# Multiplying gamma into all four chunks of the last row block ahead of its root, on GpSimd and VectorE

## The chip, the cores and the metric

The kernel runs on one core of a Trainium2 chip. The metric is the device time of one execution in microseconds (us). Every kernel was run, and one execution of each was profiled. The profile names the engines PE (TensorE), DVE (VectorE), ACT (ScalarE), POOL (GpSimd) and SP (the engine that issues most DMAs here). "Chunk" means 512 of the 2048 columns of a block of 128 rows.

## The reference

```python
m, k, n = 2048, 2048, 2048          # a, b, gamma: float32
x = np.matmul(a, b)
rms = np.sqrt(np.mean(x ** 2, axis=-1, keepdims=True) + eps)
return (gamma * x / rms).astype(np.float32)
```

A row of the output cannot be scaled before the whole row of x is known, because its rms needs all 2048 columns.

## The kernel before

The kernel computes the product by a scheme of seven products for each pair of row blocks, keeps x in SBUF, and finishes each block with `x * r * gamma`, where r is one over the rms. ("The root" below is the step on ScalarE that makes the rms; "filler" is work put where VectorE would otherwise wait for it.) The change touches only the very last block of 128 rows, `rb`, whose root comes after the last matmul. This is the end of the kernel:

```python
# gam[c]: chunk c of gamma; xb: chunks 0 and 1 of the last rows, x22[0] is chunk 1
# x21[1], x22[1]: places of chunks 2 and 3; p4[1]: chunk 2, still in PSUM
def add(out, in0, in1, op=ALU.add):
    nc.vector.tensor_tensor(out=out, in0=in0, in1=in1, op=op)
def scaled_gamma(x, src, r, gamma_of_x):
    nc.vector.scalar_tensor_tensor(out=x, in0=src, scalar=r, in1=gamma_of_x,
                                   op0=ALU.mult, op1=ALU.mult)
def by_r(x, r):
    nc.scalar.activation(out=x, in_=x, func=ACTF.Copy, scale=r)
# ... cut: the seven products; chunk 0 is already multiplied by gam[0] ...
add(x22[0], p6, t[0])
square(rb, x22[0])
scaled_gamma(x_tile(ra, 1), x_tile(ra, 1), r_a, gamma_sb[:, HALF:])
nc.sync.dma_start(out=rows(ra, HALF, N), in_=x_tile(ra, 1))
# ... cut: the last products, in two halves of 256 columns ...
for h, col in enumerate(halves):
    add(x22[1][:, col], p6[h], t[1][:, col])
    # ... cut: ScalarE squares this half and sums it into half_sq[:, h] ...
# ... cut: part = half_sq[:, 0:1] + the sums of the other chunks ...
add(x22[0], x22[0], gam[1], ALU.mult)          # filler while ScalarE makes the root
r_b = inverse_rms(half_sq[:, 1:2], part)       # ScalarE root, VectorE reciprocal
x = xb[:, 0:CH]
nc.vector.tensor_scalar_mul(out=x, in0=x, scalar1=r_b)
nc.sync.dma_start(out=rows(rb, 0, CH), in_=x)
x = xb[:, CH:]
by_r(x, r_b)
nc.scalar.dma_start(out=rows(rb, CH, HALF), in_=x)
for c, x, src in ((3, x22[1], x22[1]), (2, x21[1], p4[1])):
    scaled_gamma(x, src, r_b, gam[c])
    nc.sync.dma_start(out=rows(rb, c * CH, (c + 1) * CH), in_=x)
```

Of the kernel before, what the change touches and what calls it, by code (L numbers as in the profile page):

```python
# [8 lines left out]
FP32 = mybir.dt.float32  # L9
# [4 lines left out]
ALU = mybir.AluOpType  # L14
# [3 lines left out]
def kernel(  # L18
# [13 lines left out]
    nc = tc.nc  # L32
    P = 128
    M, K = a.shape
# [5 lines left out]
    CH = 512  # L40
    NCH = N // CH
    HALF = N // 2
# [6 lines left out]
    a_pool = ctx.enter_context(tc.tile_pool(name="a_pool", bufs=2))  # L49
# [61 lines left out]
    a32 = {}  # L111
# [134 lines left out]
    def b_quarter(j, kp, r, c):  # L246
        return raw[j][kp][:, r, c * CH:(c + 1) * CH]
# [24 lines left out]
    def product(g, j, m, bank, start=True):  # L272
        for kp in range(KP):
            lhsT = {3: quarter(g, 0, 0), 4: quarter(g, 1, 1)}[m] if m in (3, 4) else s_sum[m]
            rhs = {1: lambda: sums[j][:, 0, kp, :], 2: lambda: b_quarter(j, kp, 0, 0),
                   3: lambda: sums[j][:, 1, kp, :], 4: lambda: sums[j][:, 2, kp, :],
                   5: lambda: b_quarter(j, kp, 1, 1), 6: lambda: b_quarter(j, kp, 0, 1),
                   7: lambda: b_quarter(j, kp, 1, 0)}[m]()
            nc.tensor.matmul(bank, lhsT[:, kp, :], rhs,  # L279
                             start=(start and kp == 0), stop=(kp == KP - 1),  # L280
                             skip_group_check=not start)
# [5 lines left out]
    def square(mb, src):  # L287
        c = n_sq[mb]
        n_sq[mb] += 1
        sq = sq_pool.tile([P, 2 * CH], BF16, name="sq")  # L290
        nc.scalar.activation(out=sq[:, 0:CH], in_=src, func=ACTF.Square,  # L291
                             scale=inv_sqrt_n, accum_out=msq[mb][:, c:c + 1])

    def x_tile(mb, h):


        if (mb, h) not in x_half:
            n = n_x[0]
            n_x[0] += 1
            if n < 8:  # L300
                slot = n
            else:
                g = n // 4
                slot = ((0, 4, 1, 5), (0, 1, 4, 5))[g // 2 % 2 == 0][n % 4] + 2 * (g % 2)
            x_half[mb, h] = x_slot[slot]
        return x_half[mb, h]

    def x_chunk(mb, c):
        return x_tile(mb, c // 2)[:, (c % 2) * CH:(c % 2 + 1) * CH]
# [21 lines left out]
    def rows(mb, lo, hi):  # L331
        return out[mb * P:(mb + 1) * P, lo:hi]

    def finish(mb, order=(0, 1)):
        if mb not in rms_of:
            take_rms(mb)
        r = inverse(rms_of.pop(mb))
        for h in order:
            x = x_half.pop((mb, h))
            nc.vector.scalar_tensor_tensor(  # L340
                out=x, in0=x, scalar=r, in1=gamma_sb[:, h * HALF:(h + 1) * HALF],
                op0=ALU.mult, op1=ALU.mult)
            nc.sync.dma_start(out=rows(mb, h * HALF, (h + 1) * HALF), in_=x)
# [9 lines left out]
    def new_bank():  # L353
        return ps_a.tile([P, CH], FP32, name="acc")
# [123 lines left out]
    def last_squares():  # L478

        while late:  # L480
            square(*late.pop(0))
# [109 lines left out]
    def last_group():  # L591


        g = NG - 1
        ra, rb = 2 * g, 2 * g + 1
        x11, x12, x21, x22 = ([x_chunk(mb, 2 * j + c) for j in range(2)]
                              for mb in (ra, rb) for c in range(2))
        xa, xb = x_tile(ra, 0), x_tile(rb, 0)
        gam = [gamma_sb[:, c * CH:(c + 1) * CH] for c in range(NCH)]
        gam_left = gamma_sb[:, 0:HALF]  # L600
        t = x22

        def partial(mb):

            m = msq[mb]
            part = stat_pool.tile([P, 1], FP32, name="part")
            nc.vector.tensor_scalar(out=part, in0=m[:, 0:1], scalar1=m[:, 1:2],
                                    scalar2=m[:, NCH:], op0=ALU.add, op1=ALU.add)
            return part

        def plus(part, mb, c):
            both = stat_pool.tile([P, 1], FP32, name="both")
            nc.vector.tensor_tensor(out=both, in0=part, in1=msq[mb][:, c:c + 1], op=ALU.add)
            return both
# [11 lines that stand above are left out]
        p4 = []  # L626
        for j in range(2):
            p5, p1 = new_bank(), new_bank()
            p4.append(new_bank())
            product(g, j, 5, p5)  # L630
            nc.scalar.copy(out=t[j], in_=p5)
            last_squares()
            product(g, j, 1, p1)
            add(t[j], p1, t[j], ALU.subtract)
            if j == 0:
                finish(2 * g - 2)
            product(g, j, 4, p4[j])
            nc.scalar.copy(out=x21[j], in_=p4[j])
            add(x11[j], t[j], x21[j])
            if j == 0:  # L640
                finish(2 * g - 1)
            product(g, j, 3, p5, start=False)
            nc.scalar.copy(out=x12[j], in_=p5)
            square(ra, x12[j])
            add(t[j], x11[j], x12[j])
            p7 = new_bank()
            product(g, j, 7, p7)
            add(x11[j], p7, x11[j])
            square(ra, x11[j])
            if j == 0:  # L650
                product(g, j, 2, p4[j], start=False)
                nc.scalar.copy(out=x21[j], in_=p4[j])
                square(rb, x21[j])
                add(t[j], t[j], x21[j], ALU.subtract)
                pre_a = partial(ra)
                add(xa, xa, gam_left, ALU.mult)
                add(x21[j], x21[j], gam[0], ALU.mult)
        r_a = inverse_rms(msq[ra][:, NCH - 1:NCH], plus(pre_a, ra, 2))
        by_r(xa, r_a)
        nc.sync.dma_start(out=rows(ra, 0, HALF), in_=xa)  # L660
        p6 = new_bank()
        product(g, 0, 6, p6)
        add(x22[0], p6, t[0])
        square(rb, x22[0])
        scaled_gamma(x_tile(ra, 1), x_tile(ra, 1), r_a, gamma_sb[:, HALF:])
        nc.sync.dma_start(out=rows(ra, HALF, N), in_=x_tile(ra, 1))
        product(g, 1, 2, p4[1], start=False)
        add(t[1], t[1], p4[1], ALU.subtract)
        square(rb, p4[1])
        pre_b = partial(rb)  # L670

        half_sq = stat_pool.tile([P, 2], FP32, name="n2")
        halves = [slice(0, CH // 2), slice(CH // 2, CH)]
        p6 = [new_bank()[:, 0:CH // 2] for _ in halves]
        for bank, col in zip(p6, halves):
            for kp in range(KP):
                nc.tensor.matmul(bank, s_sum[6][:, kp, :], b_quarter(1, kp, 0, 1)[:, col],
                                 start=(kp == 0), stop=(kp == KP - 1))
        for h, col in enumerate(halves):
            add(x22[1][:, col], p6[h], t[1][:, col])  # L680
            sq = sq_pool.tile([P, 2 * CH], BF16, name="sq")
            nc.scalar.activation(out=sq[:, 0:CH // 2], in_=x22[1][:, col], func=ACTF.Square,  # L682
                                 scale=inv_sqrt_n, accum_out=half_sq[:, h:h + 1])
        part = stat_pool.tile([P, 1], FP32, name="part")
        nc.vector.tensor_scalar(out=part, in0=half_sq[:, 0:1], scalar1=pre_b,
                                scalar2=msq[rb][:, 2:3], op0=ALU.add, op1=ALU.add)
        add(x22[0], x22[0], gam[1], ALU.mult)
        r_b = inverse_rms(half_sq[:, 1:2], part)
        x = xb[:, 0:CH]
        nc.vector.tensor_scalar_mul(out=x, in0=x, scalar1=r_b)  # L690
        nc.sync.dma_start(out=rows(rb, 0, CH), in_=x)
        x = xb[:, CH:]
        by_r(x, r_b)
        nc.scalar.dma_start(out=rows(rb, CH, HALF), in_=x)
        for c, x, src in ((3, x22[1], x22[1]), (2, x21[1], p4[1])):
            scaled_gamma(x, src, r_b, gam[c])
            nc.sync.dma_start(out=rows(rb, c * CH, (c + 1) * CH), in_=x)

    for g in range(G0, NG - 1):
        for j in range(2):  # L700
# [36 lines left out]
```

## Time and profile before

| | |
|---|---|
| Time of the kernel before | 224.7 us median of 3 runs (224.52 to 224.71) |
| Profiled span | 222.6 us |
| Reciprocal of the last rows starts | 216.16 us |
| First and last of the four stores issued | 216.87 and 218.19 us |
| Last packet of the last store | 221.06 us (from the trace's record of DMA packets) |

The page's first part gives each engine's busy time, with its share of the span in brackets and the number of its instructions:

```profile
PE 211.1 (95%) x1043; PEld 98.6 (44%) x1043; DVE 161.8 (73%) x324; ACT 129.1 (58%) x272; POOL 24.5 (11%) x49
```

PE fills the span up to the last matmul, and the change does not touch it. What it touches is the stretch after it. Here is the timeline of that stretch. Its columns are the start in us, the duration in us, the engine, the line of the source, the operation, what it writes and reads with the shapes, the count, and in brackets the idle time before it with its releaser:

```profile
214.72 0.42 DVE L617 TENSOR_TENSOR x<-acc,x 128x256 f32<-128x256 f32 x1 [0.26 <-PE acc L677]
215.29 0.42 ACT L682 ACTIVATE sq<-x 128x256 bf16<-128x256 f32 x1
215.48 0.68 DVE L617 TENSOR_TENSOR x<-x,gamma_sb 128x512 f32<-128x512 f32 x1
215.83 0.29 ACT L328 ACTIVATE rms<-n,part 128x1 f32<-128x1 f32 x1
216.16 0.16 DVE L322 RECIPROCAL r<-rms 128x1 f32<-128x1 f32 x1
216.35 0.72 ACT L624 ACTIVATE x<-x,r 128x512 f32<-128x512 f32 x1 [0.23 <-DVE r L322]
216.35 0.48 DVE L690 TENSOR_SCALAR x<-x,r 128x512 f32<-128x512 f32 x1
216.76 0.74 DVE L620 SCALAR_TENSOR_TENSOR x<-x,r,gamma_sb 128x512 f32<-128x512 f32 x1
216.87 0.33 SPq L691 DMA_DIRECT2D out_dram<-x  x1
217.11 0.36 ACTq L694 DMA_DIRECT2D out_dram<-x  x1
217.42 0.74 DVE L620 SCALAR_TENSOR_TENSOR x<-acc,r,gamma_sb 128x512 f32<-128x512 f32 x1
217.53 1.05 SPq L697 DMA_DIRECT2D out_dram<-x  x2
```

The half add at 214.72 is the last thing that waits for a matmul. From there a serial path leads through the square, the root and the reciprocal. Then four chunks are scaled and stored, and VectorE's two instructions of 0.74 us are the longest part of it. The chain of waits says the same: its last pieces (start, duration, what) are these.

```profile
216.35 0.48 DVE x L690
216.84 0.66 DVEq L732
217.50 0.66 DVE x L620
```

This invites the reading that 0.66 us of VectorE work is worth removing. But the chain shown here stops at the last compute instruction, at 218.16, while the span goes on for 4.4 us. The busy time by stretches shows what fills them. Its last two columns are the busy share of the core's 16 DMA engines and what they moved, in GB/s:

```profile
core 0: us, PE busy (x) PEld busy (x) DVE busy (x) ACT busy (x) POOL busy (x), PEclk, DMA share, GB/s
217.50:218.00 0.50, 0.00 (x0) 0.00 (x0) 0.50 (x2) 0.00 (x0) 0.00 (x0) 1.00 0.59 217
218.00:218.50 0.50, 0.00 (x0) 0.00 (x0) 0.16 (x1) 0.00 (x0) 0.00 (x0) 1.00 1.04 385
218.50:219.00 0.50, 0.00 (x0) 0.00 (x0) 0.00 (x0) 0.00 (x0) 0.00 (x0) 1.00 1.05 340
219.00:219.50 0.50, 0.00 (x0) 0.00 (x0) 0.00 (x0) 0.00 (x0) 0.00 (x0) 0.82 1.12 316
219.50:220.00 0.50, 0.00 (x0) 0.00 (x0) 0.00 (x0) 0.00 (x0) 0.00 (x0) 0.50 0.98 332
220.00:220.50 0.50, 0.00 (x0) 0.00 (x0) 0.00 (x0) 0.00 (x0) 0.00 (x0) 0.50 1.08 324
220.50:221.00 0.50, 0.00 (x0) 0.00 (x0) 0.00 (x0) 0.00 (x0) 0.00 (x0) 0.50 0.49 184
```

From 218.0 on the DMA engines are full (a share of 1.0; it can exceed 1 because the recorded times of packets overlap), and they stay full until about 220.4.

### The profile page before, as it was taken

How to read it: one execution, taken by the hardware profiler on the slowest of the kernel's cores; microseconds unless marked ns; L12 is line 12 of the kernel's file. 1: busy time of each engine (PE TensorE's matmuls, PEld its weight loads, DVE VectorE, ACT ScalarE, POOL GpSimd, SP SyncE). 2: the span in 40 equal slices, each digit the busy share in tenths (PEclk: the TensorE clock that was granted, in tenths of full speed). 3: DMA queues.
4: the chain of work that ended last, by engine and by line, in shares of the span. 5: the costliest groups of instructions: out<-in, count | busy, mean ns of one | idle time of the engine just before them, and what ended most of it. 6: DMA issues, size and time to landing. Idle time of an engine off the chain costs nothing.

```text
span 222.6 us, 3026 instructions
## 1 busy us (share of the span) xinstructions
PE 211.1 (95%) x1043; PEld 98.6 (44%) x1043; DVE 161.8 (73%) x324; ACT 129.1 (58%) x272; POOL 24.5 (11%) x49
## 2 busy tenths in 40 slices
PE   7899999999999999999999999999999999999950
PEld 2445444444454444444444444444444444444430
DVE  2427557983999989978949298837994589587692
ACT  3110002807698895799646985699478954334570
POOL 7534232300000001000100002000200000000000
PEclk9999999999999999999999999999999999999997
DMA  6999999999973499818889259945994794044045
GB/s 184 223 202 209 203 208 211 212 303 259 327 280 159 188 272 292 310 72 226 276 228 400 58 174 222 366 151 143 246 368 168 97 282 189 0 188 193 0 190 188
DMA packets 36176, 47.13 MB, mean 212 GB/s; under 512 B 21952, under 2 KB 26048, under 8 KB 34496
## 3 DMA queue, kind: packets, MB, share of 16 engines
q0 software_dynamic: 9648, 23.33, 41.6%
q1 hardware_dynamic: 26080, 22.29, 33.0%
q10 hardware_dynamic: 432, 1.31, 2.0%
q8 instruction: 8, 0.13, 0.2%
q14 instruction: 8, 0.07, 0.1%
HBM read 34.60 MB, written 16.78 MB: 231 GB/s over the span
## 4 chain that ended last, share of the span: by engine, by line
PE 83%; DMA 8%; DVE 2%; POOL 2%; issue 1%; ACT 1%; DVEq 0%; ACTq 0%; POOLq 0%
PE acc L279 63%; PE acc L350 18%; DMA b<-in_b_dram 8%; POOL early L106 1%; DVE x L617 1%; POOL b L100 1%; DVE x L620 1%; PE tbank L179 1%; PE tbank L382 1%; PE tbank L165 1%; ACT sq L291 0%; DVEq L732 0%; ACT sq L682 0%; DVE x L690 0%; DVE r L322 0%
## 5 line engine op out<-in xcount | busy, mean ns | idle before, releaser
L279 PE MATMUL acc<-b,s 128*128 128x512 bf16 x376 | 83.3, 379 | 0.0
L279 PEld LDWEIGHTS <-s 128*128 128x128 f16 x472 | 46.2, 98 | 55.7 <-DVE s L244 0.2
L350 PE MATMUL acc<-b,head_at 128*128 128x512 bf16 x240 | 55.1, 379 | 0.6 <-DMA b<-in_b_dram 0.4
L291 ACT ACTIVATE sq<-x 128x512 bf16<-128x512 f32 x62 | 39.1, 631 | 10.9 <-DVE x L520 5.1
L340 DVE SCALAR_TENSOR_TENSOR x<-x,r,gamma_sb 128x1024 f32<-128x1024 f32 x28 | 34.7, 1282 | 0.8
L209 ACT ACTIVATE sq<-a 128x1024 bf16<-128x1024 f32 x24 | 25.4, 1057 | 16.8 <-DMA a<-in_a_dram 16.4
L350 PEld LDWEIGHTS <-head_at 128*128 128x128 bf16 x240 | 22.9, 98 | 26.7 <-issue 1.1
L393 ACT COPY x<-acc 128x512 f32<-128x512 f32 x11 | 5.9, 591 | 25.1 <-PE acc L350 25.1
L231 ACT ACTIVATE head_at<-a,s 128x2048 f16<-128x2048 f32 x10 | 19.9, 1990 | 0.0
L279 PEld LDWEIGHTS <-at_even 128*128 128x128 f16 x96 | 9.4, 98 | 11.5 <-issue 0.4
L279 PEld LDWEIGHTS <-head_at 128*128 128x128 f16 x96 | 9.4, 98 | 11.3
L100 POOL DMA_DIRECT2D b<-in_b_dram x15 | 10.6, 708 | 16.0 <-DMA b<-in_b_dram 13.2
L217 DVE TENSOR_SCALAR s<-norm 128x1 f32<-128x1 f32 x12 | 1.8, 150 | 14.3 <-ACT norm L212 14.2
L244 DVE TENSOR_TENSOR s<-at_even 128x1024 f16<-128x1024 f16 x15 | 9.7, 684 | 2.8 <-DMA at_even<-head_at 2.8
L291 ACT ACTIVATION_READ_ACCUMULATOR sq<-x 128x1 f32 x62 | 11.7, 188 | 0.0
L279 PE MATMUL acc<-t_left,s 128*128 128x512 bf16 x48 | 11.3, 379 | 0.0
L279 PE MATMUL acc<-early,s 128*128 128x512 bf16 x48 | 11.3, 379 | 0.0
L279 PE MATMUL acc<-early,at_even 128*128 128x512 bf16 x48 | 11.0, 379 | 0.0
L279 PE MATMUL acc<-t_left,at_even 128*128 128x512 bf16 x48 | 10.9, 379 | 0.0
L509 ACT COPY x<-acc 128x512 f32<-128x512 f32 x10 | 5.7, 575 | 8.9 <-PE acc L279 8.9
L279 PE MATMUL acc<-t_left,head_at 128*128 128x512 bf16 x48 | 10.8, 379 | 0.0
L279 PE MATMUL acc<-early,head_at 128*128 128x512 bf16 x48 | 10.8, 379 | 0.0
(86 smaller groups left out, 205.8 us busy)
## 6 DMA issues: line engine op xcount, KB each, us to landing
out_dram<-x SPq DMA_DIRECT2D x30, 512.0 KB, 3.1
a<-in_a_dram POOLq DMA_DIRECT2D x12, 1024.0 KB, 8.5
b<-in_b_dram POOLq DMA_DIRECT2D x15, 512.0 KB, 17.1
early<-in_a_dram POOLq DMA_DIRECT2D x7, 256.0 KB, 14.8
early<-in_b_dram ACTq DMA_DIRECT2D x2, 512.0 KB, 5.9
gamma_sb<-in_gamma_dram POOLq DMA_DIRECT2D x1, 1024.0 KB, 19.9
out_dram<-x SPq DMA_DIRECT2D x3, 256.0 KB, 3.5
early<-in_a_dram SPq DMA_DIRECT2D x1, 512.0 KB, 5.7
```

The lines of the kernel that those rows point to most:

```text
L100: nc.gpsimd.dma_start(out=raw[j][kp], in_=b[kp * W2:(kp + 1) * W2, j * HALF:(j + 1) * HALF].rearrange("(t p) n -> p t n", p=P))
L106: nc.gpsimd.dma_start(out=ah(kp), in_=a[0:HB * P, kp * W2:(kp + 1) * W2].rearrange("(r p) k -> p r k", p=P))
L165: nc.tensor.matmul(view[:, t, r, :], ah(kp)[:, r, t * P:(t + 1) * P], identity, is_transpose=True, start=(t == 0 and r == 0), stop=(t == 1 ...
L209: nc.scalar.activation(out=junk, in_=a32[mb][:, h * HALF:(h + 1) * HALF], func=ACTF.Square, scale=2.0 ** -8, accum_out=n2[:, h:h + 1])
L231: nc.scalar.activation(out=a16[mb], in_=a32.pop(mb), func=ACTF.Copy, scale=factor.pop(mb))
L244: nc.vector.tensor_tensor(out=s_sum[s], in0=x, in1=y, op=op)
L279: nc.tensor.matmul(bank, lhsT[:, kp, :], rhs, start=(start and kp == 0), stop=(kp == KP - 1), skip_group_check=not start)
L291: nc.scalar.activation(out=sq[:, 0:CH], in_=src, func=ACTF.Square, scale=inv_sqrt_n, accum_out=msq[mb][:, c:c + 1])
L340: nc.vector.scalar_tensor_tensor(out=x, in0=x, scalar=r, in1=gamma_sb[:, h * HALF:(h + 1) * HALF], op0=ALU.mult, op1=ALU.mult)
L350: nc.tensor.matmul(bank, head_at[:, kt, r, :], head_rhs(c, kt), start=(kt == 0), stop=(kt == KT - 1))
L393: copy(out=x_chunk(*g), in_=banks[g])
L509: nc.scalar.copy(out=x21, in_=p2)
```

## The change

The intent is to leave nothing but a plain multiplication by r for after the root. Gamma goes into chunk 1 and chunk 3 on GpSimd and into chunk 2 on VectorE, in the place of the old filler. After r, VectorE scales chunks 0 and 3 and ScalarE scales chunks 1 and 2.

```diff
         square(rb, x22[0])
+        nc.gpsimd.tensor_tensor(out=x22[0], in0=x22[0], in1=gam[1], op=ALU.mult)
 ... cut ...
+        x3 = a_pool.tile([P, K], FP32, name="a32")[:, 0:CH]
 ... cut ...
             add(x22[1][:, col], p6[h], t[1][:, col])
+            nc.gpsimd.tensor_tensor(out=x3[:, col], in0=x22[1][:, col], in1=gam[3][:, col],
+                                    op=ALU.mult)
 ... cut ...
-        add(x22[0], x22[0], gam[1], ALU.mult)
+        add(x21[1], p4[1], gam[2], ALU.mult)
         r_b = inverse_rms(half_sq[:, 1:2], part)
-        x = xb[:, 0:CH]
-        nc.vector.tensor_scalar_mul(out=x, in0=x, scalar1=r_b)
-        nc.sync.dma_start(out=rows(rb, 0, CH), in_=x)
-        x = xb[:, CH:]
-        by_r(x, r_b)
-        nc.scalar.dma_start(out=rows(rb, CH, HALF), in_=x)
-        for c, x, src in ((3, x22[1], x22[1]), (2, x21[1], p4[1])):
-            scaled_gamma(x, src, r_b, gam[c])
-            nc.sync.dma_start(out=rows(rb, c * CH, (c + 1) * CH), in_=x)
+        done = [(0, xb[:, 0:CH]), (1, xb[:, CH:]), (3, x3), (2, x21[1])]
+        for n, (c, x) in enumerate(done):
+            if n % 2 == 0:
+                nc.vector.tensor_scalar_mul(out=x, in0=x, scalar1=r_b)
+            else:
+                by_r(x, r_b)
+            queue = nc.scalar if n == 3 else nc.sync
+            queue.dma_start(out=rows(rb, c * CH, (c + 1) * CH), in_=x)
```

## The prediction

> **What bounds it now.** The page gives PE 95% of the span; the change leaves all of that alone. It touches only what follows the last product, so I read the timeline of the last 10 us.
>
> - The last matmul group feeds two half adds on VectorE (the second 214.72 to 215.14). Then ScalarE squares it (215.29, ended by its accumulator read at 215.80), takes the root (215.83 to 216.12), and VectorE takes the reciprocal (216.16 to 216.32). This part is serial.
> - A filler multiply by gamma (0.68 us, 215.48 to 216.16) sits on VectorE just before the reciprocal and ends 0.04 us after the root.
> - After r: chunk 0 scaled on VectorE (0.48 us), chunk 1 on ScalarE (0.72), then chunks 3 and 2 as scalar_tensor_tensor on VectorE (0.74 each, about 0.66 apart). The stores are issued at 216.87, 217.11, 217.53 and 218.19.
> - But the stretch-by-stretch table shows the DMA engines at a busy share of 1.0 from 218.0 to 220.4, at 310 to 400 GB/s, with a ramp-down to 221.0. All four stores (1.05 MB) drain in 3.3 us from the first data at about 217.65. The remaining 1.6 us of the span are the ending.
>
> So the tail after r is bounded by when the *first* store is issued, plus 1.05 MB at about 330 GB/s; the compute for chunks 3 and 2 runs inside it.
>
> **What the change does.**
> - Chunk 1 times gamma moves from VectorE to GpSimd, free once ScalarE has squared it (about 213.3). No GpSimd multiply is in the trace; the Trainium skill, "GPSIMD Engine Reference" § 3.1, gives 4497 ns for a 2048-element fp32 tensor_tensor. Estimate from it: 1.2 us for 512, 0.65 for each 256 half of chunk 3. GpSimd then runs about 213.4 to 214.6, to 215.25, to 215.9: 0.4 us before r.
> - The filler in front of the reciprocal becomes chunk 2 times gamma, from PSUM: 0.67 to 0.69 us by the trace's other PSUM adds. Same place, same length: r stays at 216.3 and the first store at 216.87.
> - After r: two scalings of 0.48 on VectorE (to about 217.3) and two of 0.72 on ScalarE (to about 217.8). Last issue about 217.8 instead of 218.19: compute ends 0.35 to 0.45 us earlier.
>
> **How much is critical.** The chain of waits ends in that last scalar_tensor_tensor, so 0.4 us looks like the gain. I don't expect it: the queue is already backlogged when the last store is issued, so the same bytes drain from the same start. Only the ramp at the end can shrink: 0 to 0.2 us. Expected 224.55 us, range 224.05 to 225.0. Chances: faster by over 2% 0.01, within 2% 0.98, slower by over 2% 0.01.
>
> **What would show it.** Reciprocal within 0.1 us of 216.16; first store at about 216.87; last issue about 0.4 us earlier; last store's landing less than 0.2 us earlier, with time from issue to landing of the last store grown from 2.5 to about 2.9 us; DMA share near 1.0 without a gap from 217.8.
>
> **What would make it wrong.**
> - GpSimd and VectorE share an SBUF port pair, held exclusively (the Trainium skill, "SBUF — State Buffer" § "SBUF: two separate sides") when the VectorE op has two SBUF inputs or a two-port mode. The half adds and the filler have one PSUM input, so should not collide. If the small [128,1] ops do, or GpSimd is twice as slow as estimated and runs into the scaling of chunk 0 at 216.35, r or the first store slips 0.3 to 1 us: about 225.
> - GpSimd's first multiply carries a start-up cost of microseconds: chunk 1 is late, and the time grows by 1 us or more.
> - The drain is less bound by bandwidth than I read: up to 0.4 us gained, 224.2.

## The result, and the profile after

The changed kernel took 224.26 us (median of 4 runs, 224.12 to 224.36), and the kernel before 224.61 us (median of 4, 224.16 to 224.71). The ratio is 0.9995 with a 95% interval of 0.998 to 1.0009, so the two are the same within the noise. A ratio in this text is taken from the record. For the experiments it is, within 0.0002, the mean time of one kernel's runs over that of the other's, so it is not quite the ratio of the medians quoted. Here the means of the runs listed give 0.9988 (three of the four runs of the kernel before are those of the table above); both lie in the interval. The measured time lies in the predicted range, but it proves little: the range also holds the 224.2 us that the prediction gave for the case in which its reading of the tail is wrong, and 224.26 is nearer to that than to the expected 224.55. What decides is the trace. A second set of 6 runs gave 0.9997 (0.9973 to 1.0021).

The timeline of the changed kernel's end, in the same columns:

```profile
213.38 1.27 POOL L665 TENSOR_TENSOR x<-x,gamma_sb 128x512 f32<-128x512 f32 x1 [53.09 <-ACT sq L291]
214.61 0.42 DVE L617 TENSOR_TENSOR x<-acc,x 128x256 f32<-128x256 f32 x1 [0.26 <-PE acc L679]
214.62 1.40 POOL L683 TENSOR_TENSOR a<-x,gamma_sb 128x256 f32<-128x256 f32 x2
215.38 0.68 DVE L617 TENSOR_TENSOR x<-acc,gamma_sb 128x512 f32<-128x512 f32 x1
216.06 0.16 DVE L322 RECIPROCAL r<-rms 128x1 f32<-128x1 f32 x1
216.25 0.49 DVE L696 TENSOR_SCALAR x<-x,r 128x512 f32<-128x512 f32 x1
216.31 1.34 ACT L624 ACTIVATE x<-x,r 128x512 f32<-128x512 f32 x2 [0.29 <-DVE r L322]
216.66 0.48 DVE L696 TENSOR_SCALAR a<-a,r 128x512 f32<-128x512 f32 x1
216.77 0.81 SPq L700 DMA_DIRECT2D out_dram<-x  x2
217.67 0.40 SPq L700 DMA_DIRECT2D out_dram<-a  x1
217.68 0.37 ACTq L700 DMA_DIRECT2D out_dram<-x  x1
```

GpSimd's three multiplies end at 216.02, 0.23 us before the first scaling. The compute does what was intended: the last store is issued at 217.68 instead of 218.19. The whole trace lies 0.1 us earlier than that of the kernel before, and did so already at 98 us, far ahead of the change. So I count from the start of the half add that the last matmul releases (214.72 before, 214.61 after). Counted so, the reciprocal starts at 1.44 and 1.45 us, the first store is issued at 2.15 and 2.16, the last one at 3.47 and 3.07, and the last packet ends the data at 6.34 and 6.20. The last issue came 0.40 us earlier and the end of the data 0.14 us earlier. By the trace's record of landings (when a store reports that it is done) the last one came at 6.93 and 6.71, and the span ended at 7.89 and 7.71, so 0.22 and 0.18 us earlier.

The stretches of the changed kernel show why: the DMA engines fill up at the same place and stay full.

```profile
217.50:218.00 0.50, 0.00 (x0) 0.00 (x0) 0.00 (x0) 0.15 (x1) 0.00 (x0) 0.50 0.77 287
218.00:218.50 0.50, 0.00 (x0) 0.00 (x0) 0.00 (x0) 0.00 (x0) 0.00 (x0) 0.50 1.06 381
218.50:219.00 0.50, 0.00 (x0) 0.00 (x0) 0.00 (x0) 0.00 (x0) 0.00 (x0) 0.50 1.07 365
219.00:219.50 0.50, 0.00 (x0) 0.00 (x0) 0.00 (x0) 0.00 (x0) 0.00 (x0) 0.50 1.07 291
219.50:220.00 0.50, 0.00 (x0) 0.00 (x0) 0.00 (x0) 0.00 (x0) 0.00 (x0) 0.50 0.98 356
220.00:220.50 0.50, 0.00 (x0) 0.00 (x0) 0.00 (x0) 0.00 (x0) 0.00 (x0) 0.50 0.94 357
220.50:221.00 0.50, 0.00 (x0) 0.00 (x0) 0.00 (x0) 0.00 (x0) 0.00 (x0) 0.50 0.17 62
```

The DMA view gives the packets of each queue, the MB they moved, and the time they took as a share of 16 engines over the window. The window is 217.2 to 222.6, 5.4 us. First the kernel before:

```profile
q1 hardware_dynamic: 432, 0.79, 44.0%
q10 hardware_dynamic: 144, 0.26, 14.7%
```

Then the changed kernel:

```profile
q1 hardware_dynamic: 432, 0.79, 40.4%
q10 hardware_dynamic: 144, 0.26, 15.7%
```

The same packets took 58.7% of 5.4 us before, which is 3.17 us on each engine, and 56.1% after, which is 3.03 us. These 0.14 us are as much as the gain at the end of the data. The engines did not wait much less: from the first packet to the last it took 3.37 us before and 3.21 after (table below), so the time beyond that of the packets is 0.20 and 0.18 us. The packets themselves were a little faster. This is a mean over the 16 engines; the trace does not tell which engine ended last.

### The profile page after: what moved, and what is told of

Read it like the earlier page. It is cut to its first block, busy times and chain, and to the rows that moved or that the text cites. A ratio compares the mean times of both kernels' runs of the same rounds, so it can differ in the third digit from the quotient of the medians.

```text
span 222.3 us, 3034 instructions
## 1 busy us (share of the span) xinstructions
PE 211.9 (95%) x1043; PEld 98.7 (44%) x1043; DVE 160.8 (72%) x323; ACT 129.7 (58%) x273; POOL 27.2 (12%) x52
## 4 chain that ended last, share of the span: by engine, by line
PE 83%; DMA 8%; POOL 2%; DVE 2%; ACT 1%; issue 1%; ACTq 0%; POOLq 0%
PE acc L279 63%; PE acc L350 18%; DMA b<-in_b_dram 8%; POOL early L106 1%; DVE x L617 1%; POOL b L100 1%; PE tbank L179 1%; PE tbank L382 1%; PE tbank L165 1%; DVE x L620 1%; ACT sq L291 0%; ACT x L624 0%; ACT sq L686 0%; DVE r L322 0%; ACT rms L328 0%
## 5 line engine op out<-in xcount | busy, mean ns | idle before, releaser
L393 ACT COPY x<-acc 128x512 f32<-128x512 f32 x11 | 5.9, 592 | 25.0 <-PE acc L350 25.0
L121 POOL COPY pace<-x 128x1 f32<-128x1 f32 x4 | 0.7, 185 | 88.7 <-DVE x L525 88.7
L244 DVE TENSOR_TENSOR s<-head_at 128x1024 f16<-128x1024 f16 x15 | 9.8, 686 | 1.5 <-DMA head_at<-head_at 1.5
```

Of the source, the lines that this page charges most:

```text
L244: nc.vector.tensor_tensor(out=s_sum[s], in0=x, in1=y, op=op)
L393: copy(out=x_chunk(*g), in_=banks[g])
```

## The experiments

My theory was that the end is set by when the *first* store is issued and by how long the DMA engines then need for 1.05 MB. Call it the drain theory. The main rival was that the end follows the issue of the *last* store by a fixed time, so that all compute up to it is on the critical path. A second question was the GpSimd work: was it safe, and was it needed? All edits are against the changed kernel. This table has all runs, in us from the start of the last half add. "Drain" runs from the start of the first packet to the last packet, and "slow" counts the packets of these stores that took over 120 ns (given for 2 KB packets; most take 84). Both come from the trace's records of single packets.

| kernel | reciprocal | first issue | last issue | drain | last packet | slow |
|---|---|---|---|---|---|---|
| before | 1.44 | 2.15 | 3.47 | 3.37 | 6.34 | 82 |
| changed | 1.45 | 2.16 | 3.07 | 3.21 | 6.20 | 50 |
| changed, again | 1.43 | 2.14 | 3.05 | 3.21 | 6.18 | 54 |
| chunk 0 stored early | 1.43 | 2.43 | 3.05 | 2.65 | 5.91 | 55 |
| last store late | 1.43 | 2.14 | 3.57 | 3.36 | 6.33 | 72 |
| r late | 1.95 | 2.65 | 3.56 | 3.24 | 6.71 | 53 |
| no GpSimd | 2.56 | 3.26 | 4.16 | 3.28 | 7.37 | 52 |
| two stores | 1.43 | 2.48 | 2.87 | 2.76 | 6.07 | - |
| two scalings, four stores | 1.43 | 2.49 | 3.39 | 3.03 | 6.35 | 15 |
| GpSimd long | 1.43 | 2.94 | 3.84 | 3.39 | 7.16 | 73 |
| quarter, then the rest | 1.43 | 2.14 | 2.76 | 2.86 | 5.83 | - |
| two stores, split | 1.43 | 2.33 | 2.84 | 2.76 | 5.91 | - |
| chunks in order 0 1 2 3 | 1.43 | 2.14 | 3.05 | 3.23 | 6.20 | 52 |
| one queue | 1.44 | 2.15 | 3.55 | 3.42 | 6.40 | 71 |

In every row the first packet starts 0.82 to 0.83 us after the first issue. So the last column but one is first issue + 0.83 + drain, within rounding; given the constant 0.83, this sum holds by the way the drain is measured and is no test of the theory. The test is whether the drain stays the same when the last issue moves. The last packet follows the *last* issue by anything from 2.8 us (last store late) to 3.3 us (GpSimd long). The rival's fixed time does not exist.

### Chunk 0 stored before r

```diff
+        nc.sync.dma_start(out=rows(rb, 0, CH), in_=xb[:, 0:CH])     # before r_a's chain
 ...
-            queue.dma_start(...)
+            if n > 0:
+                queue.dma_start(...)
```

> The changed kernel, but chunk 0 of the last rows is stored unscaled about 6 us before r (a wrong result, on purpose): every byte is still written once, the compute is the same, and only three stores (0.79 MB) are left after r. The issue of the last store stays at about 217.7. Theory (the drain of the backlog bounds the end: first store's data plus bytes at about 327 GB/s, from 3.21 us for 1.05 MB in the changed kernel): first data at about 217.8 instead of 217.6, 2.4 us of drain, last byte at about 220.2 instead of 220.8, so 0.5 to 0.6 us less. Rival (the end follows the last issue by a fixed 3.1 us): last byte still at 220.8, no gain.

The last issue stayed where it was (3.05), and the last packet came at 5.91 instead of 6.20, so 0.29 us earlier. The ratio to the kernel before was 0.9982 (0.9967 to 0.9997). The rival, which allowed no gain, is out. But the gain was only half of what I expected. I had costed the 128 packets taken away at the average rate of the whole drain, 0.8 us. The drain got shorter by 0.56 us only. Most 2 KB packets take 84 ns, so an estimate for 128 of them is 128 x 84 / 16 = 0.67 us of each engine. The DMA view comes near it: 44.4% of 5.4 us, 2.40 us, in place of 3.03. The slow packets stayed: 55 here, 50 in the changed kernel. That they and an uneven end of the engines are the rest of the miss is argued and not tested. Against this stands the first issue, 0.27 us later because chunk 1 comes from ScalarE.

### Only the last store late

```diff
+                if n == 3:
+                    nc.scalar.copy(out=spill, in_=gam[0])     # read by nobody
                 by_r(x, r_b)
```

> The changed kernel with one extra 128x512 ScalarE copy ahead of chunk 2's scaling, so only the last store is issued about 0.6 us later (218.3 instead of 217.7); r and the other three stores are untouched. Theory: the backlog hides it; the last byte moves by 0 to 0.25 us. Rival (end = last issue plus a fixed time): plus 0.6 us.

The last issue moved from 3.07 to 3.57, and the last packet from 6.20 to 6.33. Of 0.50 us of delay 0.13 us came through. This run has the tail of the kernel before in nearly every number: last issue 3.57 against 3.47, drain 3.36 against 3.37, last packet 6.33 against 6.34. Its DMA view, in the same window, has the packet time of the kernel before too: 58.7%, which is 3.17 us.

```profile
q1 hardware_dynamic: 432, 0.79, 44.3%
q10 hardware_dynamic: 144, 0.26, 14.4%
```

So a late last store, put back alone, gives back the changed kernel's gain at the end of the data (0.13 of 0.14 us). Its time was 224.38 us, ratio 1.0 (0.9986 to 1.0015).

### r late

```diff
         add(x21[1], p4[1], gam[2], ALU.mult)
+        add(spill, p4[1], gam[2], ALU.mult)     # read by nobody
```

> The changed kernel with one extra 128x512 VectorE multiply (0.60 us start to start) ahead of the reciprocal, so r and with it all four stores come 0.6 us later. Theory and rival both: plus 0.6 us at the end. It is the yardstick for the run with only the last store late: a delay of the same size, placed ahead of the first store, has to be paid in full.

```profile
215.80 0.68 DVE L617 TENSOR_TENSOR a<-acc,gamma_sb 128x512 f32<-128x512 f32 x1
216.40 0.15 DVE L322 RECIPROCAL r<-rms 128x1 f32<-128x1 f32 x1
```

The reciprocal came 0.50 us later, not 0.60. Here the first filler (215.20), the second and the reciprocal follow each other at 0.60 us. In the changed kernel the reciprocal starts 0.68 us after its one filler, 0.03 us after the root ends, so about 0.08 us of the added filler fits into that wait. The last packet moved from 6.20 to 6.71, by 0.51 us. In the profile the delay was paid in full. A delay of the same size costs 0.51 us ahead of the first store and 0.13 us ahead of the last. The timed runs cannot tell the two apart so sharply: this kernel took 224.55 us, ratio 1.0012 (0.9997 to 1.0028), the one with the last store late 1.0 (0.9986 to 1.0015).

### The gamma products without GpSimd

```diff
-        nc.gpsimd.tensor_tensor(out=x22[0], in0=x22[0], in1=gam[1], op=ALU.mult)
-            nc.gpsimd.tensor_tensor(out=x3[:, col], in0=x22[1][:, col], in1=gam[3][:, col], ...)
+        add(x22[0], x22[0], gam[1], ALU.mult)
+        add(x3, x22[1], gam[3], ALU.mult)
         add(x21[1], p4[1], gam[2], ALU.mult)
```

> The changed kernel with the three GpSimd multiplies made by VectorE instead (two of 128x512, in the filler's place ahead of the reciprocal). Theory: r comes 1.2 to 1.35 us later and the whole of it shows in the time, about 0.5% slower than the changed kernel, though the work after r is the same as there. Rival (early products are worth their time wherever they run): within 0.3 us of the changed kernel.

The reciprocal came 1.11 us later (2.56) and the last packet 1.17 us later (7.37). The time was 225.32 us, ratio to the kernel before 1.0043 (1.0025 to 1.0061). With VectorE alone the idea loses: the products would stand ahead of the first store. Offloading to GpSimd is what makes the change harmless.

### GpSimd kept busy past r

```diff
+        nc.gpsimd.tensor_tensor(out=spill, in0=gam[0], in1=gam[3], op=ALU.mult)  # after chunk 3's
```

> The changed kernel with one more GpSimd multiply (128x512, 1.27 us, read by nobody) behind chunk 3's, so that GpSimd is busy from about 213.4 to 217.3, over the VectorE scalings of chunk 0 (216.25) and chunk 3. If the shared port pair is an exclusive lock between GpSimd and VectorE's two-port scalings: chunk 0's scaling waits until about 217.3, the first store goes out up to 1 us later and the time grows by 0.5 to 1 us. If not: nothing moves by more than 0.1 us, and the 0.2 us between the end of GpSimd's work and r was no risk.

The timeline of this kernel:

```profile
216.09 1.26 POOL L689 TENSOR_TENSOR a<-gamma_sb 128x512 f32<-128x512 f32 x1
216.16 0.16 DVE L322 RECIPROCAL r<-rms 128x1 f32<-128x1 f32 x1
216.36 1.28 DVE L698 TENSOR_SCALAR x<-x,r 128x512 f32<-128x512 f32 x1
217.56 0.47 DVE L698 TENSOR_SCALAR a<-a,r 128x512 f32<-128x512 f32 x1
```

VectorE's scaling of chunk 0 took 1.28 us instead of 0.49. It ended 0.29 us after GpSimd, which ended at 217.35. The small reciprocal ran through under GpSimd undisturbed, and GpSimd itself was not slowed (1.26 us). The last packet came 0.96 us later, the time was 225.3 us, ratio 1.0039 (1.0019 to 1.0059). So the 0.23 us that the changed kernel leaves between GpSimd's end and the first scaling are a real margin. The Trainium skill, "SBUF — State Buffer", section "SBUF: two separate sides", says that the port pair is an exclusive lock between GpSimd and a VectorE instruction in a two-port mode or with two SBUF inputs. This trace agrees, as far as it goes: the scaling was held (1.28 us for 0.49), but the trace does not show in which mode it ran. The other direction can be seen in the kernel "quarter, then the rest" below: there GpSimd's multiply started under a VectorE instruction with two SBUF inputs and took 2.19 us instead of 1.27.

```profile
212.13 1.28 DVE L620 SCALAR_TENSOR_TENSOR x<-x,r,gamma_sb 128x1024 f32<-128x1024 f32 x1
212.35 2.19 POOL L667 TENSOR_TENSOR a<-x,gamma_sb 128x512 f32<-128x512 f32 x1 [52.41 <-DVE x L617]
```

### Two stores of half rows

```diff
+        right = a_pool.tile([P, K], FP32, name="a32")[:, 0:HALF]
+        x2, x3 = right[:, 0:CH], right[:, CH:]          # chunks 2 and 3 side by side
 ...
+        nc.vector.tensor_scalar_mul(out=xb, in0=xb, scalar1=r_b)
+        nc.sync.dma_start(out=rows(rb, 0, HALF), in_=xb)
+        by_r(right, r_b)
+        nc.scalar.dma_start(out=rows(rb, HALF, N), in_=right)
```

> The changed kernel with chunks 2 and 3 made in one buffer, and after r one VectorE scaling of the left half (128x1024), one ScalarE scaling of the right half, and two stores of 512 KB (4 KB for each row) in place of four of 256 KB (2 KB for each row). Theory (end = first store's data + bytes / rate) with the rate that the two earlier 512 KB stores had (399 GB/s from 214 to 216 us): first issue at about 216.97 instead of 216.77, first data at 217.8, drain 2.63 us instead of 3.21, last byte at about 220.4 instead of 220.8: 0.4 us gained. Rival (the size of the row pieces does nothing to the rate): 0.2 us lost.

The first store was issued later than expected, at 2.48 (VectorE's scaling of 128x1024 took 0.75 us). The drain fell from 3.21 to 2.76 us, and the last packet came at 6.07, 0.13 us earlier than in the changed kernel, where I had hoped for 0.4. The time was 224.12 us, ratio 0.9986 (0.9966 to 1.0006), which is no difference clear of noise. The direction was right and the size was not. Against the changed kernel the drain was 0.45 us shorter and the first store 0.32 us later. Against what I expected, the first store was 0.12 us too late and the drain 0.13 us too long (2.76 and not 2.63), so both halves share in the miss.

### Two scalings, four stores

The same kernel with each of the two stores cut into two of 512 columns.

> As the two-store kernel in buffers and scalings, but with four stores of 256 KB. It tells the rate apart from the fewer instructions. Theory: first issue at 216.97, drain about 3.2 us at 327 GB/s, last byte at about 221.0: 0.2 us slower than the changed kernel and 0.6 us slower than with two stores. Rival (the gain of two stores is from fewer scalings): as fast as two stores.

The drain was 3.03 us and the last packet came at 6.35, 0.28 us later than with two stores. The time was 224.76 us, ratio 1.0013 (0.9997 to 1.003). So the gain of two stores is not from the fewer scalings, which this kernel has too. But the drain was also shorter than the changed kernel's, and I had expected no difference. Only 15 of its packets were slow. So 0.18 of the 0.45 us by which two stores shorten the drain come without larger row pieces, from something that this kernel shares with the two-store one: chunks 2 and 3 side by side in one buffer, or the two wide scalings and the times at which they release the stores. No run separates these. The other 0.27 us come with two stores in place of four, which changes the row pieces, the number of stores and the last issue (2.87 and not 3.39) at once.

### A quarter first, then the rest; and two stores, each half scaled by both engines

```diff
 # a quarter, then the rest: chunks 1 to 3 side by side in `rest`
+        nc.vector.tensor_scalar_mul(out=x, in0=x, scalar1=r_b)               # chunk 0
+        nc.sync.dma_start(out=rows(rb, 0, CH), in_=x)
+        by_r(rest[:, 0:896], r_b)
+        nc.vector.tensor_scalar_mul(out=rest[:, 896:], in0=rest[:, 896:], scalar1=r_b)
+        nc.scalar.dma_start(out=rows(rb, CH, N), in_=rest)
 # two stores, split
+        for x, lo, queue in ((xb, 0, nc.sync), (right, HALF, nc.scalar)):
+            nc.vector.tensor_scalar_mul(out=x[:, 0:640], in0=x[:, 0:640], scalar1=r_b)
+            by_r(x[:, 640:], r_b)
+            queue.dma_start(out=rows(rb, lo, lo + HALF), in_=x)
```

> A version meant to beat both: chunk 0 scaled on VectorE and stored at once (first issue 0.71 us after the reciprocal's start, as in the changed kernel), chunks 1 to 3 made side by side in one buffer, scaled by ScalarE (896 columns) and VectorE (640) and sent as one 768 KB store (6 KB for each row) at about 1.32 us after the reciprocal's start. Theory (end = first data + bytes / rate, with the 380 GB/s that the two-store kernel's large pieces had): from the reciprocal's start to the last byte about 4.3 to 4.4 us, against 4.75 in the changed kernel, 4.90 before and 4.64 with two stores: 0.5 us less than before. Rival (the last issue plus a fixed 2.8 us): 1.32 + 2.8 = 4.1 us.

> The two-store kernel with each half scaled by both engines (640 columns VectorE, 384 ScalarE), so the first store is issued at about 0.88 us after the reciprocal's start instead of 1.05. Theory: the end comes earlier by just that, 4.47 us after the reciprocal's start instead of 4.64. Rival (the last store's issue sets it): about the same gain, since the last store moves too; this run is a candidate rather than a test.

From the reciprocal's start to the last packet the first took 4.40 us (expected 4.3 to 4.4; the rival 4.1) and the second 4.48 us (expected 4.47). Both are correct, and both beat the kernel before by less than half a per cent: 223.78 us, ratio 0.9966 (0.9953 to 0.9978), and 223.71 us, ratio 0.9963 (0.9949 to 0.9976), with the kernel before at 224.51 us. Their last packets come 0.51 and 0.43 us earlier than in the kernel before. The medians gained 0.73 and 0.80 us. Part of the difference is the choice of the profiled execution: both are the slowest, or nearly so, of their six (223.99 and 223.87 us, spans of 222.2 and 222.1 where most others have 221.9 to 222.0). The slow ends of the intervals, gains of 0.49 and 0.54 us, come near the gains at the last packet. More than that I can't explain from these profiles. The stretches of the split kernel show the drain at its best:

```profile
218.00:218.50 0.50, 0.00 (x0) 0.00 (x0) 0.00 (x0) 0.00 (x0) 0.00 (x0) 1.00 1.03 410
218.50:219.00 0.50, 0.00 (x0) 0.00 (x0) 0.00 (x0) 0.00 (x0) 0.00 (x0) 1.00 1.03 418
219.00:219.50 0.50, 0.00 (x0) 0.00 (x0) 0.00 (x0) 0.00 (x0) 0.00 (x0) 0.60 0.99 402
219.50:220.00 0.50, 0.00 (x0) 0.00 (x0) 0.00 (x0) 0.00 (x0) 0.00 (x0) 0.50 1.02 410
```

It holds 402 to 418 GB/s, where the changed kernel fell to 291 between 219.0 and 219.5 at the same full share.

### Chunk order, and one queue

One run swaps chunks 2 and 3 after r. The other puts the last store on the same queue as the others. Both were run once (224.33 and 224.55 us), so their state is unknown.

> The changed kernel with chunks 2 and 3 swapped after r (VectorE scales 2, ScalarE scales 3), issue times untouched. In the changed kernel 50 of 512 store packets took over 120 ns (0.3 us of 3.21 in sum over 84 ns each), with two ops and four stores 15. If the slow packets belong to the order of the chunks (1 followed by 3), they fall to about 15 and the last byte comes 0.15 us earlier, 4.6 us after the reciprocal's start. If they belong to the timing of the issues: 4.75 us as in the changed kernel.

> The changed kernel with the last store on the same queue as the others, so its issue comes about 0.4 us later (218.1 instead of 217.7) behind the third's. Theory (the backlog hides most of a late last issue, as 0.14 of 0.51 us showed): 4.75 to 4.90 us from the reciprocal's start to the last byte. Rival (fixed time from the last issue): 5.15 us.

With the order 0 1 2 3 nothing changed: last packet at 6.20, 52 slow packets. The order of chunks 2 and 3 is not what makes packets slow. With one queue the last issue came at 3.55, 0.48 us later, and the last packet at 6.40, 0.20 us later. That is 4.96 us from the reciprocal's start, a little above the 4.90 that I had given, and below the rival's 5.15.

The slow packets follow a pattern only in part. Four kernels whose last store is issued at least 0.4 us after the third one (before, last store late, GpSimd long, one queue) had 71 to 82 of them and drains of 3.36 to 3.42 us. Those that issue the last two within 0.2 us had 50 to 55, and the ones among them with four stores after r had drains of 3.21 to 3.28 us. But "two scalings, four stores" breaks it: its last store, too, is issued 0.47 us after the third, with the same order of chunks and queues as in "GpSimd long", and it had 15 slow packets where that one had 73. It is the only one of the four-store kernels in which chunks 2 and 3 lie side by side in one buffer. Two queues are not needed for slow packets either, since "one queue" had 71. Why a packet takes up to 0.22 us there is open: no run isolates it.

## Why the prediction was right

- **What bounds the tail.** Right in the main. The test with the same delay at two places shows it best (0.51 us against 0.13). But the drain is not a constant: with the same bytes in four stores it took 3.03 to 3.42 us, and about a quarter of a delay of the last store came through (0.13 of 0.50).
- **r and the first store.** Right: reciprocal at 216.06 (predicted within 0.1 of 216.16), and the same distance from the last half add in both kernels.
- **GpSimd.** The estimate was 1.2 us and 0.65 for each half, from the Trainium skill, "GPSIMD Engine Reference", section 3.1. The trace shows 1.27 us, and 1.40 for the two halves. The end was put at 215.9 and came at 216.02, so the margin ahead of the first scaling was 0.23 us and not 0.4. The worry about the port pair was justified: the run with GpSimd kept busy paid 0.96 us. The small [128,1] instructions and those with a PSUM input were not held (the half add took 0.42 us and the filler 0.68 in both kernels).
- **The last issue.** Right: 0.40 us earlier from the same anchor, predicted 0.35 to 0.45.
- **The gain.** Right in size: 0.14 us at the end of the data, predicted 0 to 0.2 (0.22 by the last landing, just above). The term that carries it was named wrongly, so that the size was right is partly luck. I said that "only the ramp at the end can shrink". In the DMA view the packets' own time fell by 0.14 us, from 3.17 to 3.03, of the 0.16 us by which the drain became shorter. There were fewer slow packets, 50 instead of 82, and putting the last store late again brought the count back to 72 and the packets' time to 3.17 us.
- **A misreading.** I gave 2.5 us as the last store's time from issue to landing. It was the smallest of the four in the profile, and it belongs to the first store. By the packets the last store took 2.87 us before and 3.13 after: it grew by 0.26 us, from another base, where I expected about 0.4.

## What to carry to other kernels

When a kernel ends in a burst of stores, look at the DMA share after the last instruction before shortening the compute. Where the engines are full before the last store is issued, expect work taken out between the first and the last store to be mostly lost: here 0.40 us of it gave 0.14, while 0.50 us ahead of the first store cost 0.51. The gain was found with two stores in place of four (4 KB of each row in both, or 2 KB and then 6) and an early first one, which gave 0.34 to 0.37% where the moved multiplies alone gave nothing clear of noise. Which part of that is due to the larger row pieces is not shown. Work given to GpSimd should end before a VectorE instruction that it can hold up begins (0.96 us was lost here), so know the margin and test it by making the work longer.

## What the Trainium skill lacked or had wrong

- "GPSIMD Engine Reference", section 3.1, has a measured two-input fp32 add only at 2048 elements (4497 ns), with a rate for each element but no fixed part for small tiles. Here 512 elements took 1.27 us and two of 256 took 1.40 us together, so as an estimate about 0.14 us fixed and 2.2 ns for each element (worked out from these two). A quarter of 4497 ns, as an estimate, would be 1.12 us.
- "SBUF — State Buffer" has rules by inputs and modes for the lock between VectorE and GpSimd, but names no [128,1] VectorE instruction. A reciprocal (0.16 us) and a two-scalar add (0.27 us) ran at their usual length under it.
- "DMA: Bandwidth & Descriptors", section "Latency and other measured facts", gives about 600 ns to the first byte for stores issued from SP or ACT. Here the first packet started 0.82 to 0.83 us after the start of the issue, in all fourteen profiles. The issue itself takes 0.33 us, so it is 0.50 us after its end; the section does not say from which moment it counts.
- None of the pages that I read has the slow packets: with the DMA engines full, 15 to 82 of 512 packets of 2 KB took 0.12 to 0.22 us instead of 84 ns. The cause is open.
